# Moving the transposes of an attention-score kernel from TensorE to VectorE, with two more early loads and two load pieces cut into 125 and 3 partitions

## Chip, cores and metric

The kernel runs on one core of a Trainium2 chip. The metric is the device time of one execution in microseconds (us), given as the median of several runs.

## The reference

```python
# q, k: (8, 12, 1024, 64) float32
def reference(q, k):
    return np.einsum('bhid,bhjd->bhij', q, k).astype(np.float32)   # (8, 12, 1024, 1024)
```

There are 96 heads. Each reads 0.52 MB and writes 4.19 MB, in all 50.33 MB read and 402.65 MB written.

## The kernel before

The heads are worked in 25 blocks: two of two heads, then 23 of four heads. A block of four has four load pieces of 512 KB (q and k of two pairs of heads), each 128 partitions of one 4 KB row. A piece is cast to float16 by GpSimd (POOL). TensorE then transposes it in tiles of 128x128 into PSUM and VectorE (DVE) copies the tiles out:

```python
in_pool = ctx.enter_context(tc.tile_pool(name="in_pool", bufs=8))
out_pool = ctx.enter_context(tc.tile_pool(name="out_pool", bufs=4))
...
def cast(self, n):
    pin(nc.gpsimd.tensor_copy(out=self.halves[n % 2][:, :, n // 2],
                              in_=self.raw[n].rearrange("p (r d) -> p r d", d=D)))
...
def transpose(self, a, x):
    t_ps = pt_pool.tile([P, NT, P], F16, tag="pt")
    for t in range(NT):
        rows = self.halves[x][:, a * NT + t]
        pin(nc.tensor.transpose(t_ps[:, t], rows, ident))
    ...
    pin(nc.vector.tensor_copy(out=dst, in_=src))
```

A head is then 16 matmuls, eight copies of 128x1024 from PSUM (three on VectorE, five on ScalarE, which the profile calls ACT), and one store of 4 MB. The stores go out on the SyncE (SP) queue, the loads of the stream on the ScalarE queue, one per head:

```python
def scores(self, n, side):
    ...
    o_sb = out_pool.tile([P, NT, S], F32, tag="out")
    for t in range(NT):
        ps = po_pool.tile([P, S], F32, tag="po")
        for j in range(2):
            js = slice(j * 512, (j + 1) * 512)
            pin(nc.tensor.matmul(ps[:, js], qT[cs, g, t], kT[cs, g, js]))
        if t in (1, 4, 6):
            pin(nc.vector.tensor_copy(out=o_sb[:, t], in_=ps))
        else:
            pin(nc.scalar.copy(out=o_sb[:, t], in_=ps))
        if t in side:
            side[t]()                      # transposes of the next block
    pin(nc.sync.dma_start(out=of[self.first + n]..., in_=o_sb...))
...
for n in range(4):                         # early loads of block 3
    blocks[3].load(n, (nc.sync, nc.scalar)[n % 2])
```

Of the kernel before, what the change touches and what calls it, by code (L numbers as in the profile page):

```python
# [11 lines left out]
P = 128  # L12


@with_exitstack
def kernel(
    ctx: ExitStack,
    tc: tile.TileContext,
    q: bass.AP,
    k: bass.AP,  # L20
    out: bass.AP,
):
    nc = tc.nc

    B, H, S, D = q.shape
    NT = S // P
    BH = B * H
    GMAX = 2
    assert D == 64 and NT == 8 and BH % (2 * GMAX) == 0







    qf = q.rearrange("b h s d -> (b h s) d")
    kf = k.rearrange("b h s d -> (b h s) d")
    of = out.rearrange("b h i j -> (b h) i j")

    sizes = [1, 1] + [GMAX] * (BH // (2 * GMAX) - 1)
    assert 2 * sum(sizes) == BH

    consts = ctx.enter_context(tc.tile_pool(name="consts", bufs=1))
    ident = consts.tile([P, P], F16)

    in_pool = ctx.enter_context(tc.tile_pool(name="in_pool", bufs=8))
    half_pool = ctx.enter_context(tc.tile_pool(name="half_pool", bufs=2))
    tr_pool = ctx.enter_context(tc.tile_pool(name="tr_pool", bufs=2))
    out_pool = ctx.enter_context(tc.tile_pool(name="out_pool", bufs=4))  # L50
    pt_pool = ctx.enter_context(
        tc.tile_pool(name="pt_pool", bufs=2, space=bass.MemoryType.PSUM)
    )
    po_pool = ctx.enter_context(
        tc.tile_pool(name="po_pool", bufs=3, space=bass.MemoryType.PSUM)
    )


    pin = tc.keep_in_program_order

    class Block:
        def __init__(self, first, G):
            self.first, self.G, self.R = first, G, 8 * G
            self.elems = self.R * D
            self.raw = [None] * 4


        def load(self, n, eng, raw=None):
            if raw is None:
                x_sb = in_pool.tile([P, self.elems], F32, tag="x")  # L70
                raw = x_sb
            self.raw[n] = raw
            start = (self.first + n // 2 * self.G) * S
            src = (qf, kf)[n % 2][start : start + self.G * S]
            pin(eng.dma_start(out=raw, in_=src.rearrange("(p r) d -> p (r d)", p=P)))  # L75

        def place(self, half_sb, at):
            n = 2 * self.elems
            self.halves = [
                half_sb[:, x * half_sb.shape[1] // 2 + at :][:, :n].rearrange(  # L80
                    "p (r h d) -> p r h d", h=2, d=D
                )
                for x in range(2)
            ]

        def cast(self, n):
            pin(
                nc.gpsimd.tensor_copy(  # L88
                    out=self.halves[n % 2][:, :, n // 2],
                    in_=self.raw[n].rearrange("p (r d) -> p r d", d=D),  # L90
                )
            )

        def alloc(self):
            self.qT = tr_pool.tile([P, GMAX * S], F16, tag="qT")
            self.kT = tr_pool.tile([P, GMAX * S], F16, tag="kT")

        def transpose(self, a, x):
            G, pp = self.G, P // self.G
            t_ps = pt_pool.tile([P, NT, P], F16, tag="pt")  # L100
            for t in range(NT):
                rows = self.halves[x][:, a * NT + t]
                pin(nc.tensor.transpose(t_ps[:, t], rows, ident))  # L103

            if x == 0:
                dst = self.qT[:, : G * S].rearrange(
                    "c (g t m a) -> c g t m a", g=G, t=NT, a=G
                )[:, :, :, :, a]
                src = t_ps.rearrange("c t (g m) -> c g t m", g=G)
            else:  # L110
                dst = self.kT[:, : G * S].rearrange(
                    "c (g m a t) -> c g m a t", g=G, a=G, t=NT
                )[:, :, :, a]
                src = t_ps.rearrange("c t (g m) -> c g m t", g=G)
            pin(nc.vector.tensor_copy(out=dst, in_=src))  # L115


        def scores(self, n, side):
            half, g = divmod(n, self.G)
            cs = slice(half * D, (half + 1) * D)  # L120
            qT = self.qT.rearrange("c (g t m) -> c g t m", t=NT, m=P)
            kT = self.kT.rearrange("c (g j) -> c g j", j=S)
            o_sb = out_pool.tile([P, NT, S], F32, tag="out")
            for t in range(NT):
# [9 lines that stand above are left out]
                    side[t]()  # L134
            pin(
                nc.sync.dma_start(
                    out=of[self.first + n].rearrange("(p t) j -> p (t j)", p=P),
                    in_=o_sb.rearrange("p t j -> p (t j)"),
                )
            )  # L140

    blocks, first = [], 0
    for G in sizes:
        blocks.append(Block(first, G))
        first += 2 * G



    early = out_pool.tile([P, NT, S], F32, tag="out")
    raw = early.rearrange("p t j -> p (t j)")  # L150
    half_elems = 2 * GMAX * NT * D
    at = 0
    for b in blocks[:3]:
        for n in range(4):
            piece = raw[:, at + n * b.elems :][:, : b.elems]
            b.load(n, (nc.sync, nc.scalar)[n % 2], piece)
        at += 4 * b.elems
    for n in range(4):
        blocks[3].load(n, (nc.sync, nc.scalar)[n % 2])
    make_identity(nc, ident)  # L160

    def to_half(some):
        half_sb = half_pool.tile([P, 2 * half_elems], F16, tag="half")
        at = 0
        for b in some:
            b.place(half_sb, at)
            at += 2 * b.elems
            for n in range(4):
                b.cast(n)

    to_half(blocks[:2])
    to_half(blocks[2:3])



    stream = [(b, n) for b in blocks[4:] for n in range(4)]

    def next_load():
        if stream:
            b, n = stream.pop(0)  # L180
            b.load(n, nc.scalar)

    blocks[0].alloc()
    for x in range(2):
        blocks[0].transpose(0, x)
    for i, b in enumerate(blocks):
        nxt = blocks[i + 1] if i + 1 < len(blocks) else None
        if nxt:
            nxt.alloc()
        heads = 2 * b.G  # L190
        for n in range(heads):
            a = n - max(0, heads - 1 - nxt.G) if nxt else -1
            side = {}
            if nxt and 0 <= a < nxt.G:
                side = {
                    1: lambda: nxt.transpose(a, 0),
                    6: lambda: nxt.transpose(a, 1),
                }
            b.scores(n, side)
            if i == n == 0:  # L200
                next_load()
            next_load()
            if nxt and a == nxt.G - 1 and 0 < i + 3 < len(blocks):
                to_half(blocks[i + 3 : i + 4])

# [29 lines left out]
```

## Time and profile before

| quantity | before |
|---|---|
| median of the runs first given | 1074.94 us |
| span of the profiled run | 1074.4 us |
| instructions counted | 6393 |
| busiest compute engine | TensorE, 69% |
| DMA mean over the span | 422 GB/s |

The chain of waits, the DMA row and the tail of the span are shown in the prediction. Each row below names the line, engine, operation, output and input tile, shapes and count; then busy us and the mean ns of one; then the idle time ahead of the group.

```profile
L103 PE MATMUL t_ps<-ident,half_sb 128*128 128x128 f16 x768 | 99.0, 310 | 6.1 <-POOL half_sb L88 6.1
...
L115 DVE COPY qT<-t_ps 128x1024 f16<-128x1024 f16 x48 | 60.6, 1263 | 7.2 <-PE t_ps L103 7.2
```

The transposes are 99.0 us of TensorE, and the copies of one side 60.6 us of VectorE. Neither number says what they are worth: that depends on what sets the end.

The second view shows what the SP queue, which issues the stores, waited for: us in total, number of waits, the longest one.

```profile
SPq L136 <- DVE o_sb L130: 848.5, 92, 10.1
...
SPq L136 <- DMA x_sb<-in_q_dram: 32.5, 2, 20.8
```

The stores wait for compute, which is the normal course here. Two waits are for a *load* of q (and one of 10.7 us for a load of k), though a store needs nothing directly from a load.

One quantity is used throughout and isn't a view of the page. The trace records the time of each increment of a transfer's semaphore. For a store there are 16, and each is taken here as the share of one of the 16 DMA engines that has landed. The **lag** of a store is the time of its last increment minus that of its median one (the eighth of the 16), so it tells how far the latest DMA engine, called the late engine from here on, is behind an ordinary one. For the last store of the kernel before it is 14.1 us.

### The profile page before, as it was taken

How to read it: one execution, taken by the hardware profiler on the slowest of the kernel's cores; microseconds unless marked ns; L12 is line 12 of the kernel's file. 1: busy time of each engine (PE TensorE's matmuls, PEld its weight loads, DVE VectorE, ACT ScalarE, POOL GpSimd, SP SyncE). 2: the span in 40 equal slices, each digit the busy share in tenths (PEclk: the TensorE clock that was granted, in tenths of full speed). 3: DMA queues.
4: the chain of work that ended last, by engine and by line, in shares of the span. 5: the costliest groups of instructions: out<-in, count | busy, mean ns of one | idle time of the engine just before them, and what ended most of it. 6: DMA issues, size and time to landing. Idle time of an engine off the chain costs nothing.

```text
span 1074.4 us, 6393 instructions
## 1 busy us (share of the span) xinstructions
PE 743.6 (69%) x2304; PEld 267.3 (25%) x2304; DVE 463.7 (43%) x384; ACT 477.2 (44%) x481; POOL 100.7 (9%) x106
## 2 busy tenths in 40 slices
PE   7977677676776757667676676767767676678740
PEld 2322222222222212222222222222222222223210
DVE  4645354452534535345353443434434444445420
ACT  4545444444444434444443544444444443544530
POOL 4100101010010100101010010100101010000000
PEclk9965555555555555555555555555555555555555
DMA  9999999999999999999999999999999999999993
GB/s 332 430 429 433 429 433 432 428 431 433 429 432 431 431 427 436 429 428 435 431 429 434 427 431 434 427 432 434 426 433 433 429 430 432 432 431 429 436 432 170
DMA packets 28257, 453.42 MB, mean 422 GB/s; under 512 B 3136, under 2 KB 3136, under 8 KB 15936
## 3 DMA queue, kind: packets, MB, share of 16 engines
q1 hardware_dynamic: 14976, 405.81, 87.7%
q10 hardware_dynamic: 13248, 47.19, 11.0%
q8 instruction: 18, 0.29, 0.1%
q14 instruction: 15, 0.12, 0.0%
HBM read 50.33 MB, written 402.65 MB: 422 GB/s over the span
## 4 chain that ended last, share of the span: by engine, by line
DMA 79%; PE 12%; ACT 4%; issue 0%; DVE 0%; ACTq 0%; POOL 0%; SPq 0%
DMA out_dram<-o_sb 79%; PE ps L128 12%; ACT o_sb L132 4%; PE t_ps L103 1%; DMA early<-in_q_dram 0%; DVE o_sb L130 0%; DVE kT L115 0%; ACTq L132 0%; POOL half_sb L88 0%; SPq L75 0%
## 5 line engine op out<-in xcount | busy, mean ns | idle before, releaser
L128 PE MATMUL ps<-kT,qT 64*128 64x512 f16 x1536 | 657.3, 621 | 289.8 <-ACT o_sb L132 286.4
L132 ACT COPY o_sb<-ps 128x1024 f32<-128x1024 f32 x480 | 475.9, 1013 | 554.7 <-DMA out_dram<-o_sb 347.6
L130 DVE COPY o_sb<-ps 128x1024 f32<-128x1024 f32 x288 | 352.7, 1225 | 568.9 <-DMA out_dram<-o_sb 404.5
L128 PEld LDWEIGHTS <-qT 64*128 64x128 f16 x1536 | 193.2, 134 | 687.0 <-issue 680.2
L88 POOL CAST half_sb<-x_sb 128x1024 f16<-128x1024 f32 x88 | 91.3, 1040 | 835.0 <-DMA x_sb<-in_k_dram 404.6
L103 PE MATMUL t_ps<-ident,half_sb 128*128 128x128 f16 x768 | 99.0, 310 | 6.1 <-POOL half_sb L88 6.1
L103 PEld LDWEIGHTS <-half_sb 128*128 128x128 f16 x768 | 74.1, 141 | 84.4 <-issue 62.4
L115 DVE COPY qT<-t_ps 128x1024 f16<-128x1024 f16 x48 | 60.6, 1263 | 7.2 <-PE t_ps L103 7.2
L115 DVE COPY kT<-t_ps 128x1024 f16<-128x1024 f16 x48 | 58.3, 1215 | 0.2 <-PE t_ps L103 0.2
L88 POOL CAST half_sb<-early 128x512 f16<-128x512 f32 (+1 forms) x12 | 8.7, 755 | 5.4 <-DMA early<-in_q_dram 5.4
L132 ACT ACT_TABLE_LOAD x1 | 1.3, 1283 | 8.8 <-DMA early<-in_q_dram 8.8
masks.py:199 POOL TENSOR_SCALAR_AFFINE_SELECT ident<-ident 128x128 f16<-128x128 f16 x1 | 0.3, 292 | 0.1
masks.py:197 POOL MEMSET ident<- 128x128 f16 x1 | 0.2, 204 | 0.3 <-POOLq L219 0.3
L219 POOL MEMSET const-float32-0.0<- 128x1 f32 x1 | 0.1, 98 | 0.2 <-issue 0.2
L219 POOL MEMSET const-bfloat16-1.0<- 128x1 bf16 x1 | 0.1, 101 | 0.0
L219 POOL MEMSET const-uint8-127<- 128x1 uint8 x1 | 0.1, 101 | 0.0
L219 POOL MEMSET const-float32-1.0<- 128x1 f32 x1 | 0.1, 98 | 0.0
## 6 DMA issues: line engine op xcount, KB each, us to landing
out_dram<-o_sb SPq DMA_DIRECT2D x96, 4096.0 KB, 36.7
x_sb<-in_k_dram ACTq DMA_DIRECT2D x44, 512.0 KB, 32.1
x_sb<-in_q_dram ACTq DMA_DIRECT2D x42, 512.0 KB, 32.1
early<-in_k_dram ACTq DMA_DIRECT2D x4, 256.0 KB, 5.0
early<-in_q_dram SPq DMA_DIRECT2D x4, 256.0 KB, 4.8
early<-in_q_dram SPq DMA_DIRECT2D x2, 512.0 KB, 7.3
early<-in_k_dram ACTq DMA_DIRECT2D x2, 512.0 KB, 7.4
x_sb<-in_q_dram SPq DMA_DIRECT2D x2, 512.0 KB, 9.3
```

Source lines behind the costliest of these rows:

```text
L88: nc.gpsimd.tensor_copy(out=self.halves[n % 2][:, :, n // 2], in_=self.raw[n].rearrange("p (r d) -> p r d", d=D),)
L103: pin(nc.tensor.transpose(t_ps[:, t], rows, ident))
L115: pin(nc.vector.tensor_copy(out=dst, in_=src))
L128: pin(nc.tensor.matmul(ps[:, js], qT[cs, g, t], kT[cs, g, js]))
L130: pin(nc.vector.tensor_copy(out=o_sb[:, t], in_=ps))
L132: pin(nc.scalar.copy(out=o_sb[:, t], in_=ps))
L219: nc = _bacc.Bacc("TRN2", target_bir_lowering=False, num_devices=1)
```

## The change

The intent has three parts. Blocks 3 to 24 are transposed by VectorE within blocks of 32 by 32, after GpSimd has cast the pieces into a layout in which that is enough. The hole in the DMA work before the first store is filled by two more early loads, for which the input pool gets ten buffers. And pieces n = 0 of blocks 8 and 15 are loaded as two DMAs, of 125 and of 3 partitions, so that they use fewer DMA engines.

```diff
-    in_pool = ctx.enter_context(tc.tile_pool(name="in_pool", bufs=8))
+    in_pool = ctx.enter_context(tc.tile_pool(name="in_pool", bufs=10))
...
-            pin(eng.dma_start(out=raw, in_=src.rearrange("(p r) d -> p (r d)", p=P)))
+            src = src.rearrange("(p r) d -> p (r d)", p=P)
+            for lo, hi in parts:
+                pin(eng.dma_start(out=raw[lo:hi], in_=src[lo:hi]))
...
+        def cast_quads(self, n):
+            raw = self.raw[n].rearrange("p (r h d) -> p r h d", h=2, d=32)
+            for h in range(2):
+                quad = slice(32 * (2 * (n // 2) + h), 32 * (2 * (n // 2) + h) + 32)
+                dst = self.half_sb[quad].rearrange(
+                    "p (x b r d) -> p x b r d", x=2, b=4, d=32
+                )
+                for b in range(4):
+                    pin(
+                        nc.gpsimd.tensor_copy(
+                            out=dst[:, n % 2, b], in_=raw[32 * b : 32 * b + 32, :, h]
+                        )
+                    )
+
+        def transpose_quads(self, a, x):
+            ...
+            pin(nc.vector.transpose(out=dst[:, two], in_=src[:, two]))
...
-    for n in range(4):
-        blocks[3].load(n, (nc.sync, nc.scalar)[n % 2])
+    stream = [(b, n) for b in blocks[3:] for n in range(4)]
+    def next_load(eng):
+        if stream:
+            b, n = stream.pop(0)
+            few = n == 0 and b in (blocks[8], blocks[15])
+            b.load(n, eng, parts=((0, 125), (125, P)) if few else ((0, P),))
+    for n in range(6):
+        next_load((nc.sync, nc.scalar)[n % 2])
```

Left out: the layout of qT, which follows that of kT now, and the passing of the queue to `next_load`.

More of the change, by code (lines that the diff above doesn't have):

```diff
@@ L61, with __init__ @@
     class Block:
-        def __init__(self, first, G):
+        def __init__(self, first, G, quads):
             self.first, self.G, self.R = first, G, 8 * G
@@ L65, in __init__, with load @@
             self.raw = [None] * 4
-        def load(self, n, eng, raw=None):
+            self.quads = quads
+        def load(self, n, eng, raw=None, parts=((0, P),)):
             if raw is None:
@@ L74, in load @@
             src = (qf, kf)[n % 2][start : start + self.G * S]
-            pin(eng.dma_start(out=raw, in_=src.rearrange("(p r) d -> p (r d)", p=P)))
+            src = src.rearrange("(p r) d -> p (r d)", p=P)
+            for lo, hi in parts:
+                pin(eng.dma_start(out=raw[lo:hi], in_=src[lo:hi]))
         def place(self, half_sb, at):
+            self.half_sb = half_sb
             n = 2 * self.elems
@@ L86, in cast @@
         def cast(self, n):
+            if self.quads:
+                self.cast_quads(n)
+                return
             pin(
@@ L92, in cast @@
             )
+        def cast_quads(self, n):
[12 more added lines that the diff above has]
+        def transpose_quads(self, a, x):
+            src = self.half_sb.rearrange("p (x n) -> p x n", x=2)[:, x]
+            src = src.rearrange("p (b r i) -> p b r i", b=4, i=32)
+            dst = (self.qT, self.kT)[x].rearrange(
+                "c (b i r) -> c b r i", b=4, i=32, r=self.R
+            )
+            two = slice(2 * a, 2 * a + 2)
+            pin(nc.vector.transpose(out=dst[:, two], in_=src[:, two]))
         def alloc(self):
@@ L98, in transpose @@
         def transpose(self, a, x):
+            if self.quads:
+                self.transpose_quads(a, x)
+                return
             G, pp = self.G, P // self.G
@@ L103, in transpose @@
                 pin(nc.tensor.transpose(t_ps[:, t], rows, ident))
-            if x == 0:
-                dst = self.qT[:, : G * S].rearrange(
-                    "c (g t m a) -> c g t m a", g=G, t=NT, a=G
-                )[:, :, :, :, a]
-                src = t_ps.rearrange("c t (g m) -> c g t m", g=G)
-            else:
-                dst = self.kT[:, : G * S].rearrange(
-                    "c (g m a t) -> c g m a t", g=G, a=G, t=NT
-                )[:, :, :, a]
-                src = t_ps.rearrange("c t (g m) -> c g m t", g=G)
+            dst = (self.qT, self.kT)[x][:, : G * S].rearrange(
+                "c (g m a t) -> c g m a t", g=G, a=G, t=NT
+            )[:, :, :, a]
+            src = t_ps.rearrange("c t (g m) -> c g m t", g=G)
             pin(nc.vector.tensor_copy(out=dst, in_=src))
@@ L120, in scores @@
             cs = slice(half * D, (half + 1) * D)
-            qT = self.qT.rearrange("c (g t m) -> c g t m", t=NT, m=P)
+            qT = self.qT.rearrange("c (g m t) -> c g t m", t=NT, m=P)
             kT = self.kT.rearrange("c (g j) -> c g j", j=S)
@@ L143 @@
     for G in sizes:
-        blocks.append(Block(first, G))
+        blocks.append(Block(first, G, len(blocks) > 2))
         first += 2 * G
@@ L172 @@
     to_half(blocks[2:3])
-    stream = [(b, n) for b in blocks[4:] for n in range(4)]
-    def next_load():
-        if stream:
-            b, n = stream.pop(0)
-            b.load(n, nc.scalar)
     blocks[0].alloc()
@@ L200 @@
             if i == n == 0:
-                next_load()
-            next_load()
+                next_load(nc.scalar)
+            next_load(nc.scalar)
             if nxt and a == nxt.G - 1 and 0 < i + 3 < len(blocks):
```

## The prediction

> **What bounds the kernel now.** I read the page's engine shares and slices first, then the chain of waits, then the busy times by stretch at both ends of the span, and last the arrivals of the sixteen semaphore increments of each transfer.
>
> ```profile
> span 1074.4 us, 6393 instructions
> PE 743.6 (69%) x2304; PEld 267.3 (25%) x2304; DVE 463.7 (43%) x384; ACT 477.2 (44%) x481; POOL 100.7 (9%) x106
> DMA  9999999999999999999999999999999999999993
> ...
> q1 hardware_dynamic: 14976, 405.81, 87.7%
> q10 hardware_dynamic: 13248, 47.19, 11.0%
> q8 instruction: 18, 0.29, 0.1%
> ```
>
> No compute engine passes 69%, and the DMA row is at nine tenths or more in 39 of 40 slices. Nearly all bytes are outputs.
>
> ```profile
> 430.91 37.77 DMA out_dram<-o_sb
> ...
> 468.79 1.02 ACT o_sb L132
> ...
> 469.85 4.43 PE ps L128 x10
> ...
> 474.31 1.02 ACT o_sb L132
> ...
> 475.34 37.76 DMA out_dram<-o_sb
> ```
>
> The chain repeats every 44.43 us, once per block of four heads: an output buffer comes free, the compute refills it in some 6.5 us, and its store lands 37.8 us after issue. One store of 4 MB needs about 9.7 us alone (8 rows of 32 KB per engine, 1.21 us each in the trace), so three or four stores are always waiting: a head's compute can slip by tens of us before the DMA engines run dry.
>
> ```profile
> 1050.00:1054.00 4.00, 0.00 (x0) 0.00 (x0) 0.00 (x0) 0.00 (x0) 0.00 (x0) 0.50 1.01 434
> 1054.00:1056.00 2.00, 0.00 (x0) 0.00 (x0) 0.00 (x0) 0.00 (x0) 0.00 (x0) 0.50 0.84 360
> 1056.00:1058.00 2.00, 0.00 (x0) 0.00 (x0) 0.00 (x0) 0.00 (x0) 0.00 (x0) 0.50 0.72 311
> 1058.00:1060.00 2.00, 0.00 (x0) 0.00 (x0) 0.00 (x0) 0.00 (x0) 0.00 (x0) 0.50 0.12 49
> 1060.00:1062.00 2.00, 0.00 (x0) 0.00 (x0) 0.00 (x0) 0.00 (x0) 0.00 (x0) 0.50 0.08 33
> ...
> 1068.00:1070.00 2.00, 0.00 (x0) 0.00 (x0) 0.00 (x0) 0.00 (x0) 0.00 (x0) 0.50 0.08 33
> ```
>
> This is the view to look at twice. The last two columns are the share of the 16 DMA engines and GB/s. From 1058 us the share is about one sixteenth: fifteen engines are done, and one alone works until about 1072. In the semaphore arrivals of the last store the fifteenth comes 12.3 us before the sixteenth, the middle one 14.1 us before. That lag isn't there at the start (0.5 us at 36 us); it grows evenly, 0.70 us per block, and stops growing once the compute ends at 1041 although stores still flow. So one engine carries about 14 us of work that the others don't have, tied to the execution of instructions and not to the data. **It sets the end**, and every store waits for it. The instruction queue q8 alone doesn't explain it: its 18 packets of 16 KB come every 60 us or so, and the lag grows smoothly between them.
>
> At the start there is a hole:
>
> ```profile
> 17.00:17.50 0.50, 0.50 (x7) 0.30 (x7) 0.50 (x1) 0.00 (x0) 0.00 (x0) 1.00 0.99 393
> ...
> 18.00:18.50 0.50, 0.50 (x5) 0.16 (x2) 0.50 (x1) 0.00 (x0) 0.50 (x1) 1.00 0.03 8
> 18.50:19.00 0.50, 0.50 (x2) 0.15 (x1) 0.45 (x1) 0.47 (x1) 0.50 (x2) 1.00 0.00 0
> 19.00:19.50 0.50, 0.35 (x1) 0.00 (x0) 0.11 (x1) 0.50 (x2) 0.50 (x1) 1.00 0.00 0
> ```
>
> The early loads are through at about 17.7 us, the first store is issued at 19.6: the DMA engines idle for some 1.9 us, the only such stretch after the first microseconds.
>
> **What the Trainium skill says.** "DMA: Bandwidth & Descriptors", section "Why a DMA increments its semaphore by 16 and not by 1", says that a transfer uses the largest number of engines, up to 16, that divides the slowest dimension of both sides, and on this path the lowest-numbered ones: 128 partitions use 16, 125 use 5, 3 use 3. The trace agrees for 128 (16 increments for each of 196 transfers, 3136 small packets); nothing of before shows 125 or 3. "VectorE: DVE Perf Modes", section "The three transpose paths", says that VectorE transposes only within 32 by 32 blocks, 311 ns for 128x128 of 16 bits; before has none. "GPSIMD Engine Reference", section "2. Architecture", says that each of 8 cores owns 16 partitions, so a cast of 32 partitions uses two cores and isn't shortened by having fewer partitions; the casts here have 128 partitions only. "Runtime: NRT & Kernel Launch", section "Instruction fetch mechanics", says that instructions are fetched by DMA in 16 KiB blocks; q8 agrees with 0.29 MB in 18 packets.
>
> **The change, part by part.**
> *TensorE.* Blocks 3 to 24 (22 of 25) lose their transposes: 22 x 32 = 704 matmuls and as many weight loads. At 310 ns that is up to 218 us of modelled duration, but pipelined: the group has 99.0 us for 768, so 91 us go. All of it is off the path, as the stores wait in line. Direct value: 0.
> *VectorE.* 88 copies from PSUM (1263 and 1215 ns) become 88 transposes of 1024 elements per partition. Scaling 311 ns naively by eight gives 2.5 us, an upper end; at one element per cycle like the copies it is about 1.2 us. I take 1.2 to 2.5 us: between 0 and +110 us on an engine at 43%, at most 5 us per block in a period of 44.4. Direct value: 0.
> *GpSimd.* 88 casts of 128x1024 (1040 ns) become 704 casts of 32x512. The 128x512 casts took 613 ns on average (8 of them, 4.7 us), so I estimate 0.6 us each, 430 us in all, 40% of the span, 19.6 us per block. A block's casts start when the buffer of the block two before is read, and are wanted some seven heads later, about 78 us. Off the path. Direct value: 0.
> *Six early loads instead of four, ten buffers instead of eight.* Two loads of 512 KB, 1.05 MB, move into the hole before the first store. At 430 GB/s they take 2.4 us, of which 1.9 us fit the hole: **-1.9 us**, as the engines stay busy from there to the end.
> *The two split pieces.* Normally each engine moves 8 rows of 4 KB of a piece, 8 x 0.155 = 1.2 us. A piece of 125 rows puts 25 on each of engines 0 to 4, and the 3 put one more on engines 0 to 2; engines 5 to 15 get nothing. Twice: engines 5 to 15 lose 2.4 us, engines 0 to 4 gain 2 x 17 to 18 rows, 5.3 to 5.6 us. The late engine lags the next by 12 us. If it is among 5 to 15, **-2.4 us**; if among 0 to 4, +5.3 us. No view numbers the engines. That the piece is cut so oddly, and only twice, suggests that someone meant to unload an engine above 4; I give that 85%.
> *Instructions.* If the late engine's extra work follows instructions, it shrinks. Per block TensorE goes from 192 to 128, and all engines together from about 240 to 205 (28 more casts, 64 fewer on TensorE). Of 14 us, in proportion to TensorE alone, 22/25 x 1/3 x 14 = 4.1 us go; in proportion to all, 22/25 x 15% x 14 = 1.8 us. The middle: **-3.0 us**.
> Sum: 1074.9 - 1.9 - 2.4 - 3.0 = 1067.6 us; I say 1067.5.
>
> **The rivals.**
> *Total bytes bound it, the late engine doesn't matter.* Against it: the single sixteenth in the tail. If so, only the hole is worth anything: 1073.
> *The late engine is among 0 to 4.* Then 1074.9 - 1.9 - 3.0 + 5.3 = 1075.3. Nothing in the profile speaks for or against.
> *The extra work isn't tied to instructions* but to time or stores. For it: the growth is even. Against it: it stops with the compute. Then 1070.6.
> *GpSimd becomes the bound.* It would need 44.4 / 32 = 1.39 us per small cast, over twice my estimate, since a cast that writes other partitions than it reads could be slow. Then each block takes over 44.4 us and the time is above 1090. In the start it comes closer: block 3's casts can begin at 17.7 us, take 20 us, and are wanted at about 45 us.
> *VectorE in step with the 32 KB queue.* A 2.5 us transpose beside three evictions delays a head by 5 us; the chain above has over 20 us of stores waiting. No cost.
>
> **Range and chances.** The favourable corner (hole fully used, -2.4, -4.1 and a little more) is about 1065, the one without the instruction effect 1070.6, with the wrong engine 1075. I take 1063 to 1072.5 for eight in ten. Fifteen engines finish at about 1058 in the kernel before and still have their bytes, so 2% faster (below 1053.4) is nearly excluded: 0.01. Slower by 2% needs GpSimd or VectorE at twice my figures: 0.02. The rest, 0.97, is within 2%.
>
> **What would show it.** Small casts near 0.6 us and GpSimd near 40%; VectorE transposes of 1.2 to 2.5 us; DMA at nine tenths to the end; no hole at 18 to 19 us; in the tail one engine alone for some 6 to 9 us instead of 14, with the split loads showing 5 and 3 engines' worth of data. A tail with five late engines would mean that the overload of engines 0 to 4 became the bound; a longer single tail, that the late engine is one of them. Gaps in the DMA row in mid-span would mean that casts or transposes hold up the stores. Equal tails with a shorter span would mean that the even growth of the lag was read wrongly.

## The result

| | before | after |
|---|---|---|
| median, runs of the same chip | 1074.84 us (1074.6 to 1076.18, 4 runs) | 1077.33 us (1077.06 to 1077.92, 4 runs) |
| ratio | | 1.0021, 95% interval 1.0004 to 1.0039 |

A ratio is the mean time of one kernel's runs over that of the other's of the same rounds, so it isn't quite the ratio of the medians. The change made the kernel about 2.5 us slower, where 7.4 us less had been predicted, and the time lies outside the predicted range.

The GB/s row of before (one entry for each fortieth of the span), then the page of after, engine shares and the same row:

```profile
GB/s 332 430 429 433 429 433 432 428 431 433 429 432 431 431 427 436 429 428 435 431 429 434 427 431 434 427 432 434 426 433 433 429 430 432 432 431 429 436 432 170
```

```profile
span 1075.3 us, 5595 instructions
...
PE 670.8 (62%) x1600; PEld 242.5 (23%) x1600; DVE 731.3 (68%) x384; ACT 477.3 (44%) x481; POOL 436.6 (41%) x722
...
GB/s 368 425 433 430 430 428 400 430 420 438 431 424 433 433 429 427 434 431 324 434 436 429 428 432 435 423 432 436 424 433 432 433 423 438 434 432 430 432 439 264
```

The instructions fell by 800 and no engine is near its limit. The GB/s row has two dips in mid-span that before doesn't have: 400 in the seventh slice and 324 in the nineteenth. The two split pieces land there (at 181.0 and 494.8 us). The groups of after that replace the old ones:

```profile
L114 POOL CAST half_sb<-x_sb 32x512 f16<-32x512 f32 x704 | 427.1, 607 | 499.1 <-DVE kT L126 462.4
...
L126 DVE STREAM_TRANSPOSE qT<-half_sb 128x1024 f16<-128x1024 f16 x44 | 198.4, 4510 | 0.0
```

The casts cost 607 ns, as estimated. The Trainium skill, "GPSIMD Engine Reference", section "2. Architecture", gives each of eight cores 16 partitions of its own, and the trace agrees that fewer partitions save nothing: a cast of 128x512 took 613 ns in after. A VectorE transpose costs 4.51 us, about twice the upper end of the estimate, yet VectorE as a whole stays at 68%.

Next, by stretch of time (start and end, length, busy us of PE, PEld, DVE, ACT, POOL, the granted clock, the share of the 16 DMA engines, GB/s): the old hole at the start, the second dip, and the tail.

```profile
18.50:19.00 0.50, 0.50 (x3) 0.16 (x1) 0.50 (x1) 0.06 (x1) 0.46 (x2) 1.00 0.98 393
...
485.00:490.00 5.00, 5.00 (x13) 1.89 (x12) 2.45 (x2) 3.43 (x4) 4.68 (x8) 1.00 0.52 200
490.00:495.00 5.00, 1.52 (x4) 0.49 (x3) 0.22 (x1) 0.26 (x2) 4.62 (x9) 1.00 0.47 185
...
1062.00:1064.00 2.00, 0.00 (x0) 0.00 (x0) 0.00 (x0) 0.00 (x0) 0.00 (x0) 1.00 0.84 360
1064.00:1066.00 2.00, 0.00 (x0) 0.00 (x0) 0.00 (x0) 0.00 (x0) 0.00 (x0) 1.00 0.38 164
...
1068.00:1070.00 2.00, 0.00 (x0) 0.00 (x0) 0.00 (x0) 0.00 (x0) 0.00 (x0) 1.00 0.08 33
```

The hole at 18.5 us is filled (share 0.98, before 0.00). In the second dip half of the DMA engines idle for ten microseconds. The tail is shorter, but not because the late engine comes earlier: the others come later. At 1062 to 1064 us the share is still 0.84, where before one engine had been alone since 1058. The last store's lag is 8.3 us instead of 14.1, and its last increment comes at 1073.9 us instead of 1072.8.

The waits of the SP queue in after:

```profile
SPq L167 <- DVE o_sb L161: 797.6, 83, 29.6
SPq L167 <- DMA x_sb<-in_q_dram: 82.4, 5, 30.9
...
SPq L167 <- DMA x_sb<-in_k_dram: 46.2, 4, 14.3
```

Stores now wait 82.4 + 46.2 us for loads instead of 32.5 + 10.7. The trace shows how. The DMAs of the program take eight completion semaphores in rotation. In before, where loads and stores alternate, the stores of the stream keep to four of them and the loads to the other four. The second DMA of a split piece shifts the rotation by one, so each of the next four stores takes a semaphore last used by a load, and isn't issued until that load has landed; after these four the stores have their own semaphores again. From 463.6 to 494.9 us no store was issued.

Last, the store-by-store comparison of the last increments: after is 0.1 us ahead of before at store 8 (counted from 0), 4.0 us behind at store 16 (just past the first split), and 6.0 behind at store 44 (just past the second). Near the end 1.1 us remain, because the loads run ahead and are over earlier (891 instead of 908 us).

### The profile page after: what moved, and what is told of

Its sections match the earlier page's. It is cut to its first block, busy times and chain, and to the rows that moved or that the text cites. A ratio compares the mean times of both kernels' runs of the same rounds, so it can differ in the third digit from the quotient of the medians. Undisturbed runs are those within 1.5% of the kernel's fastest.

```text
span 1075.3 us, 5595 instructions
## 1 busy us (share of the span) xinstructions
PE 670.8 (62%) x1600; PEld 242.5 (23%) x1600; DVE 731.3 (68%) x384; ACT 477.3 (44%) x481; POOL 436.6 (41%) x722
## 4 chain that ended last, share of the span: by engine, by line
DMA 71%; DVE 9%; PE 6%; ACT 3%; issue 1%; DVEq 0%; ACTq 0%; SPq 0%
DMA out_dram<-o_sb 67%; PE ps L159 6%; DMA x_sb<-in_k_dram 5%; DVE qT L126 4%; DVE o_sb L161 4%; ACT o_sb L163 3%; DVE kT L126 1%; DVEq L161 0%; ACTq L163 0%; SPq L167 0%
## 5 line engine op out<-in xcount | busy, mean ns | idle before, releaser
L114 POOL CAST half_sb<-x_sb 32x512 f16<-32x512 f32 x704 | 427.1, 607 | 499.1 <-DVE kT L126 462.4
L161 DVE COPY o_sb<-ps 128x1024 f32<-128x1024 f32 x288 | 366.5, 1288 | 302.5 <-DMA out_dram<-o_sb 193.9
L159 PEld LDWEIGHTS <-qT 64*128 64x128 f16 x1536 | 236.2, 158 | 786.3 <-issue 781.2
L126 DVE STREAM_TRANSPOSE qT<-half_sb 128x1024 f16<-128x1024 f16 x44 | 198.4, 4510 | 0.0
L126 DVE STREAM_TRANSPOSE kT<-half_sb 128x1024 f16<-128x1024 f16 x44 | 198.2, 4505 | 0.0
L140 PE MATMUL t_ps<-ident,half_sb 128*128 128x128 f16 x64 | 8.1, 311 | 6.2 <-POOL half_sb L95 6.2
L145 DVE COPY qT<-t_ps 128x1024 f16<-128x1024 f16 x4 | 4.9, 1218 | 7.3 <-PE t_ps L140 7.3
L140 PEld LDWEIGHTS <-half_sb 128*128 128x128 f16 x64 | 6.3, 142 | 11.1 <-POOL half_sb L95 6.2
L145 DVE COPY kT<-t_ps 128x1024 f16<-128x1024 f16 x4 | 4.9, 1214 | 0.0
```

Source lines behind the costliest of these rows:

```text
L114: nc.gpsimd.tensor_copy(out=dst[:, n % 2, b], in_=raw[32 * b : 32 * b + 32, :, h])
L126: pin(nc.vector.transpose(out=dst[:, two], in_=src[:, two]))
```

## The experiments

**The theories.** Two followed from these traces. *A, the gap:* the split shifts the rotation, stores are held, and the idle engines of the two dips are the loss. *B, the overload:* the late engine is one of those that the 125 partitions use, gets 17 rows of 4 KB more by each split, 17 x 0.155 = 2.6 us, and as every store waits for it, both go straight into the time: 5.3 us. For B speaks an arrival. The piece of 125 partitions posted five increments in the second dip, at 490.1, 490.4, 491.6, 491.7 and 494.8 us. The last coincides with the latest increment of the store in flight (494.7, the others by 490.9). The 3 partitions posted theirs by 491.9. So the late engine seemed to be among the five and not among the three.

The packet records of after speak for B as well. A packet is one row piece, 4 KB of a load or 32 KB of a store, or the small write of an increment. In an engine's unbroken work each packet starts 3 or 4 ns before the end recorded for the one before it. One such chain runs without a break from 485.7 to 496.8 us and holds the last increments both of that store and of the 125 partitions (written at 494.17 and 494.18 us), while the other fifteen engines begin the next store at 495.75 us. So the late engine worked right through the dip in which the others idled.

This also is where the Trainium skill bears on the case: "DMA: Bandwidth & Descriptors", section "Why a DMA increments its semaphore by 16 and not by 1", says how many engines take part and that only those post on completion. The trace agrees: 5 landing increments for 125 partitions, 3 for 3, and in the runs below 4 for 124 and 4 for 4, each time after one early increment within 1.5 us of the issue. That they are the lowest-numbered engines is the page's word; the runs can only show which of these sets contain the late engine.

Each of the four groups ran on another chip with the kernel before beside it, so a difference between two groups is less certain than a ratio to before. The kernel before took 1075.1 us (1074.81 to 1076.23) beside the first four runs, 1075.92 (1074.71 to 1076.01) beside the next four, 1076.1 (1074.74 to 1076.44) beside the three after those, and 1075.82 (1074.64 to 1076.06) beside the last.

### 1. The pieces whole

```diff
-            b.load(n, eng, parts=((0, 125), (125, P)) if few else ((0, P),))
+            b.load(n, eng, parts=((0, P),) if few else ((0, P),))
```

> The changed kernel with both pieces loaded whole again. Theory A (the late engine is above 4; the split relieves it by 2.4 us, but the stores held back behind the split load's semaphore leave it idle for 6.9 us): 1077.3 - 6.9 + 2.4 = 1072.8 us. Theory B (the late engine is 3 or 4; the split loads it by 5.3 us, and the gap in the stores costs it nothing): 1077.3 - 5.3 = 1072.0 us. Both: no slice below 420 GB/s in mid-span, and one engine alone in the tail for 12 us or more. This run doesn't tell A from B; it says what the split as a whole costs.

Measured: 1072.05 us (1071.98 to 1072.11), ratio to before 0.9969 (0.9954 to 0.9984). So the split costs 1077.33 - 1072.05 = 5.3 us, and the rest of the change is a gain: this version beats both kernels. Store by store, after falls 4.0 us behind it at the first split, with one load piece more moved by then (1.24 us), and 2.7 us more at the second, so each split costs about 2.7 us where B put 2.6. In its GB/s row and tail

```profile
GB/s 361 428 432 434 424 436 428 434 433 427 435 427 435 425 436 431 429 435 426 434 429 430 434 428 433 431 429 437 426 436 426 433 431 432 433 432 433 432 432 199
...
1056.00:1058.00 2.00, 0.00 (x0) 0.00 (x0) 0.00 (x0) 0.00 (x0) 0.00 (x0) 1.00 0.12 49
```

the dips are gone, and from 1056 us one engine in sixteen works, as in before two microseconds later. The lag is back at 12.7 us. Both theories allow this.

### 2. An even number of extra DMAs

The piece in three DMAs, of 2, 1 and 125 partitions, so that the rotation returns to where it was while the rows per engine stay.

```diff
-            ... parts=((0, 125), (125, P)) if few else ((0, P),)
+            ... parts=((0, 2), (2, 3), (3, P)) if few else ((0, P),)
```

> The same rows on the same engines, but as three DMAs of 2, 1 and 125 partitions: an even number added leaves the stores on the semaphores of stores, so no store waits for a load. Theory A: the gaps at the split loads (slices of 400 and 324 GB/s) go, and with them 6.9 us: 1070.4 us. Theory B: the gaps go, the time stays near 1077 us, as the late engine has the same rows; five engines' arrivals of the stores after a split lie 2.6 us behind the others'.

Measured: 1077.3 us (1076.81 to 1081.31), ratio 1.0026 (1.0007 to 1.0045). The time is what B said, but the run is a miss as an experiment, because the gaps didn't go. The third DMA of a piece now waits in the ScalarE queue for an earlier load's semaphore, and ScalarE with it, so the row of GB/s has its low slices later:

```profile
GB/s 361 429 428 433 430 431 434 428 434 430 428 435 432 428 429 436 428 389 413 388 409 421 437 435 430 424 438 430 425 436 431 434 429 327 435 430 428 430 428 357
```

### 3. Two halves of 64

Two DMAs again, one extra, so the rotation shifts as in after; but 64 partitions are spread evenly over 16 engines.

```diff
+            ... parts=((0, 64), (64, P)) if few else ((0, P),)
```

> Two DMAs of 64 partitions each: the stores change over to the loads' semaphores as in the changed kernel, but each engine has its 8 rows as in a whole piece. Theory A: stores are held as before, 1077 to 1080 us. Theory B: gaps may show in the DMA row, but the late engine works on through them: 1072 to 1073 us, as with whole pieces.

Measured: 1072.13 us (1071.72 to 1072.76), ratio 0.9972 (0.9955 to 0.9989). The stores were held for loads, even longer than in after (99.3 + 64.2 us against 128.6):

```profile
SPq L167 <- DMA x_sb<-in_k_dram: 99.3, 6, 30.0
SPq L167 <- DMA x_sb<-in_q_dram: 64.2, 6, 20.3
...
GB/s 364 431 430 428 432 430 435 430 428 434 428 432 434 428 433 428 423 404 434 428 431 432 429 430 432 432 432 430 430 435 426 432 427 437 434 431 431 432 432 236
```

and the time is that of whole pieces. So the holding by itself costs nothing here, and what costs 5.3 us is the uneven rows. The engines hardly idled, though: the lowest slice in mid-span is 404 GB/s, where after has 324. For a dip as deep as that one the evidence is the unbroken chain of packets shown above, and experiment 4, whose dips (375 and 360 GB/s) come with a time 3.4 us below that of after. **A falls, B stands.**

### 4. 124 and 4

These use four engines each, 0 to 3. If the late engine is 4, it is freed now instead of loaded; if 3, it is loaded more.

```diff
+            ... parts=((0, 124), (124, P)) if few else ((0, P),)
```

> 124 and 4 partitions: by the rule all 32 + 1 shares of 4 KB rows go to engines 0 to 3 (31 and 1 rows each), none to engine 4 and above. Theory A: as the changed kernel, near 1077 us, since engines above 4 are relieved alike and engines 0 to 3 have 12 us to spare for their 7.4 us. Theory B with the late engine being 4: 1072.0 - 2.5 = 1069.5 us. Theory B with the late engine being 3: 1072.0 + 7.4 = 1079.4 us.

Measured: 1073.96 us (1071.95 to 1074.67), ratio 0.9984 (0.9969 to 0.9999). This is far from the 1079.4 that engine 3, or any lower one, would have given, so with experiment 1 **the late engine is number 4**, as the page numbers them: the 125 rows use engines 0 to 4 and hurt, the 124 rows use 0 to 3 and don't hurt it. But the gain hoped for failed to come. Engines 0 to 3 got 7.4 us more than they had, and around the split

```profile
490.00:495.00 5.00, 1.29 (x4) 0.53 (x4) 2.34 (x2) 2.17 (x3) 4.26 (x7) 1.00 0.38 148
```

most engines idled while the next stores were held for the slow load. At the end the lag is 6.0 us and the fifteenth engine 1.1 us behind the last: several engines end together.

### 5. The last two loads as 124 and 4

The rotation shifts twice, close together, and only one stretch of stores can be held.

```diff
+            few = n >= 2 and b is blocks[-1]
+            ... parts=((0, 124), (124, P)) if few else ((0, P),)
```

> Blocks 8 and 15 whole again; instead the last two loads of all (block 24, second pair) go as 124 and 4 partitions, so all their rows to engines 0 to 3. After them come only stores, and a store that reuses such a load's semaphore comes four heads later, so the holding of stores should be small. If the late engine is engine 4: 1072.05 - 2 x 8 x 0.155 = 1069.6 us, and four engines' arrivals of the last stores lie 7.4 us behind the middle. If the late engine is 3 (or lower): 1072.05 + 7.4 = 1079.5 us. If above 4 (which the two runs with 125 partitions speak against): also 1069.6 us.

Measured: 1073.44 us (1072.71 to 1074.05), ratio 0.998 (0.9965 to 0.9995). The late engine was relieved: one increment, which I take for it, is 4.4 us behind the first in the last store, where it was 15.1 with whole pieces, and lands at about 1065.8 us instead of 1068.7. But four others came last, 7.6 to 8.2 us behind the first. They had first to do their extra rows, with the next stores waiting for those loads to land (60 us from issue). The identity is supported again, the time is a miss.

### 6. Early loads alone

After with whole pieces, and with the transposes of all blocks left to TensorE and the casts as they were. Against before that leaves the ten buffers and the six early loads (and q is copied from PSUM in the layout of k).

```diff
-        blocks.append(Block(first, G, len(blocks) > 2))
+        blocks.append(Block(first, G, False))
...
-            b.load(n, eng, parts=((0, 125), (125, P)) if few else ((0, P),))
+            b.load(n, eng, parts=((0, P),))
```

> Only the early loads and the ten buffers of the change; TensorE transposes all blocks (its copies write the changed kernel's order of columns), casts are whole, no piece is split. The prediction's step: -1.9 us against before, 1073.2 us. If the whole gain of the kernel without splits (-3.0 us) comes from here: 1072.1 us. If the hole isn't worth anything: 1075.1 us.

Measured: 1073.66 us (1072.94 to 1073.78), ratio 0.9981 (0.9966 to 0.9996): 2.0 us by the ratio, as predicted (1.9).

### 7. VectorE transposes and small casts alone

After, with whole pieces, eight buffers and four early loads.

```diff
-    in_pool = ctx.enter_context(tc.tile_pool(name="in_pool", bufs=10))
+    in_pool = ctx.enter_context(tc.tile_pool(name="in_pool", bufs=8))
...
-            b.load(n, eng, parts=((0, 125), (125, P)) if few else ((0, P),))
+            b.load(n, eng, parts=((0, P),))
...
-    for n in range(6):
+    for n in range(4):
```

> Only the VectorE transposes and the small casts; eight buffers and four early loads as before, no split. The prediction's step for fewer instructions: -3.0 us, 1072.1 us, and a lag of the late engine that grows about 0.55 us per block, not 0.70. If the lag isn't tied to the number of instructions: within 0.5 us of 1075.1, or -1.1 us if what e1_whole gained beyond the hole comes from here.

Measured: 1074.3 us (1073.47 to 1074.42), ratio 0.9987 (0.9972 to 1.0001): 1.4 us by the ratio, half of what was predicted, and an interval that just includes nothing at all. The lag of the last store fell from 14.1 to 13.2 us.

The parts add up: -2.0, -1.4 and +5.3 make +1.9 us, and 2.5 us was measured.

### 8. Each store as two DMAs

The version with whole pieces, each store as two DMAs of 64 partitions: were the late engine's extra work tied to DMAs, it should have grown.

```diff
+            for lo, hi in ((0, 64), (64, P)):
+                pin(nc.sync.dma_start(out=...[lo:hi], in_=...[lo:hi]))
```

> The changed kernel with whole pieces, each store as two DMAs of 64 partitions: the same rows on the same engines, 12 DMAs per block instead of 8. If the late engine's extra time comes with each DMA issued (descriptors, semaphores): its lag against the middle engine at the end grows from 12.7 to about 19 us, 1072 + 6 = 1078 us. If it comes with instructions or with time: 12.7 us and 1072 to 1073 us (96 x 16 more semaphore packets of 9 ns add 0.9 us to every engine at most).

Measured: 1161.31 us (1159.66 to 1168.96), ratio 1.0815 (1.0773 to 1.0858). A clear miss: I hadn't thought of the rotation. With two stores and one load per head, every third DMA is a load, so no semaphore is the stores' own:

```profile
SPq L169 <- DMA x_sb<-in_k_dram: 365.7, 36, 25.5
SPq L169 <- DMA x_sb<-in_q_dram: 356.1, 37, 19.1
```

722 us of waiting for loads, and the core moved 215 to 294 GB/s in five slices early on. The late engine can't be read from this run. It does show that what cost nothing twice (experiment 3) costs 8% when it happens 73 times.

### 9 and 10. Relief of engine 4 before any store is queued

Eleven buffers and seven early loads, of which the last two go as 124 and 4 (run 9); the same with all pieces whole is its control (run 10).

```diff
-    in_pool = ctx.enter_context(tc.tile_pool(name="in_pool", bufs=10))
+    in_pool = ctx.enter_context(tc.tile_pool(name="in_pool", bufs=11))
...
+            few = n in (1, 2) and b is blocks[4]          # run 9 only
+            ... parts=((0, 124), (124, P)) if few else ((0, P),)
...
-    for n in range(6):
+    for n in range(7):
```

> After with whole mid-span pieces, 11 load buffers and 7 early stream loads, of which the last two (block 4, n = 1 and 2) go as 124 and 4 partitions, before any store is in the queue. They put 48 rows of 4 KB more on engines 0 to 3 (7.4 us) and take 16 rows (2.5 us) from engines 4 to 15. Two more DMAs are an even number, so stores keep their own completion semaphores. If the late engine is 4 or higher and engines 0 to 3 have 10 us in hand at the end: 2.5 us less than the same with whole pieces, about 1069.5, and in the tail the late engine about 11 us behind the median as before but all of it earlier, or engines 0 to 3 with it. If it is one of 0 to 3: about 1079. If the holding of stores, not the rows, took the gain in the earlier 124 and 4 runs, this run shows it by having the gain.

> Control for the run before: the same 11 buffers and 7 early loads, all pieces whole. The hole before the first store is already filled with 6 early loads, so a seventh gains nothing: 1072.05, within 0.5 us of the run with whole pieces and 10 buffers.

Measured: 1073.21 us (1073.08 to 1073.46), ratio 0.9975 (0.9961 to 0.999) for run 9; 1070.96 us (1070.67 to 1071.47), ratio 0.9955 (0.994 to 0.997) for the control. Both expectations missed. The control came out fastest of all correct kernels; its interval overlaps that of experiment 1, which ran on another chip, though the runs themselves don't. The stretches of whole pieces and six early loads, of the control with seven, and of run 9, in this order:

```profile
20.50:24.00 3.50, 3.44 (x9) 1.18 (x8) 1.55 (x2) 2.57 (x4) 3.22 (x7) 1.00 0.98 248
```

```profile
20.50:24.00 3.50, 3.43 (x9) 1.21 (x8) 1.55 (x2) 2.57 (x4) 3.26 (x6) 1.00 1.19 483
```

```profile
19.00:21.50 2.50, 2.50 (x13) 1.17 (x12) 2.16 (x2) 0.73 (x1) 1.55 (x3) 1.00 0.32 110
```

With six early loads the hole at 18 us is closed, but while the first store starts the engines move only 248 GB/s; from 17 to 26 us, in stretches of half a microsecond, the control moved 0.43 MB more, an estimated 1.0 us at 430 GB/s and close to the 1.1 us that it gained. I had taken a share of 0.98 for a full stretch. In run 9 engines other than 0 to 3 ran dry instead: share 0.32 before the first store, which was issued at 21.8 us instead of 19.9, which fits that in this stretch each further DMA held its queue for over two microseconds (on ScalarE the issues were at 8.3, 10.7 and 13.3 us). From 17 to 26 us it moved 1.58 MB less than the control, an estimated 3.7 us at 430 GB/s, so more than the 2.5 us saved in rows was lost as idle time. That the late engine isn't one of 0 to 3 holds here for the third time (it would have been 1079).

### 11. Half of the compute, the same DMAs

A wrong result: each odd head's store writes the even head's result again. Matmuls and evictions halve; loads, stores, casts and transposes stay.

```diff
-            o_sb = out_pool.tile([P, NT, S], F32, tag="out")
-            for t in range(NT):
+            if n % 2:
+                o_sb = self.last
+                for t in side:
+                    side[t]()
+            else:
+                o_sb = out_pool.tile([P, NT, S], F32, tag="out")
+            self.last = o_sb
+            for t in range(0 if n % 2 else NT):
```

> Wrong result on purpose: whole pieces, and each odd head's store writes the result of the even head before it again, so matmuls, weight loads and evictions halve while loads, stores, casts and transposes stay. If the late engine's extra work follows the number of instructions executed: instructions fall from about 5600 to about 3200, and the lag of the last store's last arrival against its median falls from 12.7 to 6 to 8 us, the time to 1065 to 1067. If it follows the stores (descriptors, bytes) or time: the lag stays at 12 to 13 us and the time within 1 us of 1072. Fewer instructions fetched (0.2 MB in the instruction queue over 16 engines) are worth less than 0.1 us either way.

Measured: 1066.45 us (1066.33 to 1066.65), ratio 0.9913 (0.9896 to 0.9929).

```profile
span 1064.7 us, 3482 instructions
...
PE 329.2 (31%) x832; PEld 120.7 (11%) x832; DVE 564.3 (53%) x240; ACT 239.9 (23%) x241; POOL 436.5 (41%) x722
```

With the same transfers the time falls by 5.6 us against experiment 1, and the lag from 12.7 to 8.1 us. So the late engine's extra time does go with what is executed, not with the transfers. (The expectation's figure for fewer fetched instructions is too low: 0.2 MB at 430 GB/s is 0.5 us, not under 0.1.)

### 12. More instructions of another kind

The version with whole pieces, with each small cast of blocks 4 to 24 made twice.

```diff
+                    for _ in range(2 if self.first >= 12 else 1):
                         pin(nc.gpsimd.tensor_copy(out=dst[:, n % 2, b], in_=...))
```

> The version with whole pieces, with each small cast of blocks 4 to 24 made twice (the second writes the same again): 672 more GpSimd instructions, 5599 to 6271, everything else as it was; GpSimd goes from 41% to about 79% busy. If the late engine's extra work goes with all executed instructions, 12.7 us per 5600 gives 1.5 us more: 1073.6, lag against the median 14.2. If it goes with the matmuls and evictions alone: within 0.4 us of 1072.05, lag 12.7. If the casts now come too late (39 us of a block's 44), gaps appear in the DMA row and the time is above 1076; then the run decides nothing about the late engine.

Measured: 1073.07 us (1072.89 to 1073.86), ratio 0.998 (0.9967 to 0.9994).

```profile
PE 669.7 (63%) x1600; PEld 242.1 (23%) x1600; DVE 732.3 (68%) x384; ACT 477.1 (45%) x481; POOL 844.3 (79%) x1394
```

Only GpSimd changed, and there is no dip in the DMA row. The lag rose from 12.7 to 14.5 us (14.2 expected by count) and the time by 1.0 us (1.5 expected by count, at most 0.4 otherwise). The time alone, taken on another call than its control, would be weak; with the lag it favours the count of all instructions over that of TensorE's, but doesn't settle it.

| run | instructions | lag of the last store, us | us per 1000 |
|---|---|---|---|
| before | 6393 | 14.1 | 2.2 |
| early loads alone | 6391 | 13.7 | 2.1 |
| casts twice | 6271 | 14.5 | 2.3 |
| transposes alone | 5601 | 13.2 | 2.4 |
| whole pieces | 5599 | 12.7 | 2.3 |
| half the compute | 3482 | 8.1 | 2.3 |

The control of run 10 doesn't fit (5598 instructions, 10.3 us). There the fifteenth engine is only 4.3 us behind the last instead of 11.0, so the median isn't a clean mark in it, but that isn't a full explanation. Runs in which stores were held or rows were uneven are left out, because there the lag changes for other reasons: 10.4 us with halves (5595 instructions), 8.3 in after, 12.6 in run 9.

**What stays open: why the late engine is slow.** Instruction fetch is a candidate, and the sums speak for it: the packets of the two instruction queues after the start of the span are 0.418 MB in before, 0.360 with whole pieces, 0.213 with half the compute and 0.401 with casts twice. At one engine's rate, 32 KB in 1.21 us, that is estimated at 15.4, 13.3, 7.9 and 14.8 us, close to the lags. The steps speak against it. If one engine fetched these packets, the interval between the last increments of two successive stores should jump by some 0.6 us where a 16 KB packet falls in. With whole pieces such intervals were 11.07 us on average (9 of them) and those without any packet 11.09 (49). An ordinary engine needs 10.95. The late engine is slower steadily, by 0.14 us per store.

The packet records show what is slow. For stores 40 to 91 the chain of packets that ends with a store's last increment can be followed back where its links are unique. In these chains a packet of 32 KB took on average

| run | late engine, ns (packets) | other engines, ns (packets) |
|---|---|---|
| before | 1234 (228) | 1214 (935) |
| whole pieces | 1231 (245) | 1214 (1340) |
| half the compute | 1222 (238) | 1214 (1639) |
| casts twice | 1231 (191) | 1214 (1119) |

After the compute has ended, in before and with whole pieces, the late engine's packets take 1213 ns. With whole pieces eight packets of 17 ns more are 0.14 us per store, which is the whole difference. So the late engine needs no packets of its own to be late, fetched instructions or others: its ordinary packets are slower while instructions execute, and the prediction's "work that the others don't have" is the wrong picture. Of the 18 instruction packets of before between 400 and 1040 us, nine were moved while one of these slow packets was under way and none stands in the late engine's chains; the other nine fall where its chains are broken. Half the compute shows the effect halved. Casts made twice don't show it in this sample, which weakens experiment 12. What slows the packets stays open. One rival no run tests: every timed execution was also recorded by the profiler, instruction by instruction, so the recording itself could be what grows with the instructions.

## Why the prediction was wrong, step by step

- **The split pieces: the step that failed.** The prediction put the late engine above 4 with 85%, from what the odd cut seemed to be meant for, and so booked -2.4 us. It is engine 4 (experiments 1 and 4, and 5 and 9 agree), which the 125 partitions do use, and the term was +5.3 us (experiment 1 against after). The arithmetic for this case stood in the prediction, and its rival gave 1075.3; with the instruction term at its measured size that rival would have been 1076.9, and 1077.3 was measured. The mistake was to take a guess about an intention for evidence about the chip, while saying that no view numbers the engines.
- **Instructions: the right mechanism, the wrong size.** -3.0 us predicted, -1.4 measured (experiment 7), -1.6 by the medians of experiments 1 and 6. The prediction had computed 1.8 us for a share of all instructions and 4.1 for a share of TensorE's, and took the middle. Experiments 11 and 12 favour all instructions, so 1.8 was the term to book. Two readings behind it were off as well: by the lag as defined here the first store, at 36 us, has 1.9 us and not 0.5, and the growth in before is 0.62 us per block and not 0.70 (0.57 in experiment 7, where 0.55 was expected). And the extra is slower packets, not more work.
- **Early loads: right**, -1.9 predicted and -2.0 measured (experiment 6). That the hole was the whole loss at the start was wrong: a seventh load brought another 1.1 us (run 10).
- **One engine sets the end: right.** The split moved the time by what it put on that engine, although fifteen engines had microseconds to spare.
- **Compute off the path: right**: even with GpSimd at 79% (experiment 12) no gap opened in the DMA row. The casts were right (607 ns, 41%). The VectorE transpose was wrong, 4.51 us against at most 2.5: the figure for 128x128 didn't scale to this instruction, and whether its size or its strides are the reason no run shows. At 68% busy that cost nothing that a run shows.
- **Not foreseen: the rotation of semaphores.** The prediction didn't ask what an extra DMA does to the ones behind it. In after this cost nothing that the runs separate from the rows (experiment 3), but it spoiled experiments 2, 4, 5 and 8.
- The signs written down beforehand worked in part. Gaps in mid-span did appear, but came from held stores and not from casts or transposes. The sign for the wrong engine, a longer single tail, did not appear: at the end the last engine was alone for 5.2 us instead of 12.3, because the other engines were late too, so this sign would have spoken for the wrong case.

## What to carry to other kernels

In this kernel the transfers were spread evenly and the last store still ended with one DMA engine alone. The time was then that engine's time, and a piece cut so that its rows fall on few engines moved the time by the rows that it gave to this engine. If a trace of yours ends like this, find out the engine's number by one timed run before building on it. An additional DMA wasn't only its bytes here: it took time to issue and coupled streams that were independent, so compare what the queues wait for before and after. At the start, look at GB/s and not only at the DMA share. And look at the mean time of a packet, engine by engine, before looking for extra packets.

## What the Trainium skill lacked or had wrong

- "DMA: Bandwidth & Descriptors": the count of engines by partitions holds (5, 3, 4 and 4 landing increments for 125, 3, 124 and 4 partitions). The page doesn't tell that one engine can run late on evenly spread transfers: 14.1 us in a span of 1074 here, its packets of 32 KB taking 1234 ns instead of 1214 while instructions execute, and engine 4 if the page's numbering holds.
- "Runtime: NRT & Kernel Launch", section "Instruction fetch mechanics", calls the cost of a block boundary mostly hidden. It has nothing on what executing instructions costs the data transfers: some 2.3 us of lag on one DMA engine per 1000 instructions here. Slower ordinary packets account for it here (17 ns more for each of eight per store); what slows them stayed open.
- "VectorE: DVE Perf Modes", section "The three transpose paths", gives 311 ns for 128x128 (bf16) and nothing for larger or strided ones. Here 128x1024 of float16, eight times as much, with this kernel's strided access took 4.51 us, 14.5 times as long.
- No page that I used tells that DMAs taking completion semaphores in rotation can hold one stream for another: 31 us without a store in after, and 8% of the time with two stores per head.
